# First weight piece in two column halves, a shorter first load of mem^T, and a new order of four evacuations

## Chip, cores and metric

One core of a Trainium2 chip runs the kernel. The metric is the device time of one execution in microseconds (us); lower is better.

## What is computed

The reference is one layer of a decoder trunk on 256 tokens of width 1024. Cut to what the change touches:

```
h    = rmsnorm(x, g_pre_mix)
proj = h @ w_in                      # columns: conv B|C|V, q, k, v, memory q, three gates
o    = moba_attention(q, k, v)       # 8 heads x 64, causal, with a position bias
kv   = rmsnorm(mem, g_mem) @ w_mem_kv        # 256 memory tokens: mk | mv, 512 columns each
y_c  = softmax(qm @ mk^T * 128**-0.5) @ mv   # 4 heads x 128
```

After that come gates, an output projection, a second rmsnorm and a gated MLP with a depthwise convolution. They are not touched.

## The kernel before, in words

**Arithmetic.** Every float32 operand of a matrix product is split into two float32r parts: `hi` is a copy made by ScalarE (ACT), `lo` is the difference made by VectorE (DVE). A product is hi·hi + hi·lo + lo·hi, three matmuls on TensorE (PE). Weights are split as they are used: `split_until` (L202) makes `wh` (L211, ACT) and `wl` (L212, DVE) of one piece; there are five buffers of each, and a piece is split three pieces ahead of the block that uses it (`weights`, L215; two ahead in v's loop).

**Pieces.** All weights lie in one DRAM tensor in the order of use (`weight_pieces`, L56). Pieces 0 to 7 are the eight k-tiles of mem's value weights (128 x 512 each), 8 to 11 mem's key weights, 12 to 15 v's weights, 16 to 19 q's, 20 to 23 k's (128 x 1024 each).

**Start.** SyncE's queue issues w0, w1, ... (one DMA a piece, L410 to L420), ScalarE's queue issues two loads of `gmT` (L132): the gain of mem and k-tiles 0 and 1 of mem^T, then k-tiles 2 and 3; SyncE brings the rest. `keep_warm` (L425) runs nine matmuls on a constant while the data comes. For k-tile 0 of mem^T the DVE makes both parts (L434, L435), for the others ACT and DVE (`mem_part`, L430). Inside the block that starts at L421 the order on PE, ACT and DVE is the order in which the code is written: w0's parts, mem^T's k-tile 1, w1's parts, k-tile 2, and so on. The first product of piece 0 is L445, of the pieces after it L251 (`mm_ktile` by way of `values`, L405).

**The stage that is reordered.** After mem's values (accumulated in `pmv`), mem's keys (`mk_raw`) and v (accumulated in `pv`, L464 to L468), the block goes on: the norms of mem's rows (`rm`, L469), the parts of mem's values scaled by `rm` (`mv`, L472), the diagonal matrices of `rm` (`dg`, L296), their spread over all partitions by a matmul with ones (`spread`, L299: PE writes `sp`, L303, DVE copies it, L305), and the scaled keys (`mk`, L476, L477). There the hand-written order ends. Behind it, in the order of the code but placed by the framework's own planner, come v's parts (`vk`, L490), four blocks of q and four of k. A block (`wide_blocks`, L352) takes a PSUM bank, runs 8 matmuls with `wh` (L237) and 8 with `wl` (L239); ACT copies half of the bank (`t`, L244) and DVE adds (`y`, L245). After each second block `q_evac` (L499) makes four instructions (L502 on ACT, L503 on DVE, for two halves of the partitions).

**PSUM.** `bank()` (L112) gives tiles of the tag "mm", four buffers: the banks of `ft` (the blocks), `sp` and, later, `po` (the attention's output, L560) are all of this tag. `pmv`, `pv`, the scores and the transposes of the attention are of the tag "acc", four buffers.

Of the kernel before, what the change touches and what calls it, by code (L numbers as in the profile page):

```python
# [11 lines left out]
F32 = mybir.dt.float32  # L12
F32R = mybir.dt.float32r
BF16 = mybir.dt.bfloat16
AF = mybir.ActivationFunctionType
ALU = mybir.AluOpType
# [3 lines left out]
P = 128  # L20
# [76 lines left out]
def trunk(ctx, tc, x, mem, memT_in, weights_in, par_in, bias_in, g_post_mix, g_post_ffn, out):  # L97
# [8 lines left out]
    def tok(t):  # L106
        return slice(t * P, (t + 1) * P)

    def f32(ap):
        return ap.bitcast(F32)  # L110
# [18 lines left out]
    gp, gf, bg, cw = par[:, 0:8], par[:, 8:16], par[:, 16:40], par[:, 40:52]  # L129
    fw = par[:, 52:].rearrange("p (a b) -> p a b", a=2)  # L130
    with tc.manual_schedule(engines={mybir.EngineType.Activation}):
        for a, b in ((0, KT + 2 * S), (KT + 2 * S, KT + 4 * S)):  # L132
            nc.scalar.dma_start(gmT[:, a:b], memT_in[:, a:b])
    ident = const.tile([P, P], F32, name="ident")
    ones = const.tile([P, P], F32, name="ones")
# [34 lines left out]
    def raw_tile(g):  # L170

        if g not in lent:
            return wp.tile([P, 2048], F32, tag="raw", name="raw", bufs=RAWS)
        tag, j = lent[g]
        if tag not in lent_tiles:
            lent_tiles[tag] = sb.tile([P, 2 if tag == "C" else 1, 2048], F32, tag=tag, name="rawx")
        return lent_tiles[tag][:, j]

    def load(first, last):

        g = load_of[first]
        if len(raws) == g:
            raws.append([raw_tile(g), 0])
        o = offs[loads[g][0]]
        a, b = offs[first], offs[last] + pieces[last][2] * pieces[last][4]
        nc.sync.dma_start(raws[g][0][:, a - o:b - o], weights_in[:, a:b])
        raws[g][1] += last + 1 - first

    def load_until(n):
        for g in range(min(n, len(loads))):  # L190
# [11 lines left out]
    def split_until(n):  # L202
        while len(parts) < min(n, len(pieces)) and (
                len(parts) in extra or sum(i not in extra for i in range(freed, len(parts))) < PARTS):
            i = len(parts)
            g = load_of[i]
            load_until(ahead_of(g))
            _, _, a, _, b = pieces[i]
            o = offs[i] - offs[loads[g][0]]
            v, hi, lo = (w[:, :a * b].rearrange("p (a b) -> p a b", b=b) for w in [raws[g][0][:, o:]] + part_tiles(i))  # L210
            nc.scalar.activation(hi, v, AF.Copy)  # L211
            nc.vector.tensor_tensor(lo, v, f32(hi), ALU.subtract)  # L212
            parts.append((hi, lo))
# [44 lines left out]
    def hilo(hi, lo, src, scale=1.0):  # L258

        nc.scalar.activation(hi, src, AF.Copy, scale=scale)  # L260
        if isinstance(scale, float) and scale == 1.0:
            nc.vector.tensor_tensor(lo, src, f32(hi), ALU.subtract)
        else:
            nc.vector.scalar_tensor_tensor(lo, src, scale, f32(hi), op0=ALU.mult, op1=ALU.subtract)
# [20 lines left out]
    def rstd_row(src, name):  # L285
        ss, se, r = small("ss"), small("se"), small(name)
        junk = wk.tile([P, D], F32, tag="pT", name="junkd", bufs=2)
        nc.scalar.activation(junk, src, AF.Square, scale=D ** -0.5, accum_out=ss)
        nc.gpsimd.tensor_scalar(se, ss, EPS, None, op0=ALU.add)
        nc.gpsimd.tensor_tensor(r, se, mhalf, op=ALU.pow)  # L290
        return r
# [92 lines left out]
    def run(gen):  # L384
        for _ in gen:
            pass
# [20 lines left out]
            mm_ktile([(pv[t], 0)], wh, wl, a[:, 0, k, tok(t)], a[:, 1, k, tok(t)], k == 0, k == KT - 1)  # L407

    with tc.manual_schedule(engines={mybir.EngineType.SP}):
        for what in "w0 w1 w2 w3 m46 w4 w5 m68 w6 w7 w8 x0 x1 w9 p w10 w11 w12 w13 t0 t1".split():  # L410
            if what[0] == "m":
                a, b = (KT + int(c) * S for c in what[1:])
                nc.sync.dma_start(gmT[:, a:b], memT_in[:, a:b])
            elif what == "p":
                nc.sync.dma_start(par, par_in)
            elif what[0] == "w":
                load(int(what[1:]), int(what[1:]))
            else:
                t = int(what[1])
                nc.sync.dma_start((x_sb if what[0] == "x" else m_sb)[:, t], (x if what[0] == "x" else mem)[tok(t)])  # L420
    with tc.manual_schedule(engines={mybir.EngineType.PE, mybir.EngineType.Activation, mybir.EngineType.DVE}):  # L421
        nc.scalar.activation(small("preload"), mhalf, AF.Exp)
        pw = bank("pw")

        def keep_warm(n):  # L425
            one = nc.const_aps.tensor(1.0, (P, 512), BF16)
            for _ in range(n):
                nc.tensor.matmul(pw, one[:, :P], one, start=True, stop=True)

        def mem_part(k):  # L430
            hilo(memT[:, 0, k], memT[:, 1, k], rawT[:, k], gm[:, k:k + 1])

        keep_warm(9)
        nc.vector.tensor_scalar_mul(memT[:, 0, 0], rawT[:, 0], gm[:, 0:1])  # L434
        nc.vector.scalar_tensor_tensor(memT[:, 1, 0], rawT[:, 0], gm[:, 0:1], f32(memT[:, 0, 0]), op0=ALU.mult,  # L435
                                       op1=ALU.subtract)
        split_until(1)
        mem_part(1)
        split_until(2)
        for k in range(KT):  # L440
            wh, wl = weights(ahead=1)
            if k == 0:
                for n, (a, w) in enumerate(((0, wh), (1, wh), (0, wl))):
                    for t in range(NT):
                        nc.tensor.matmul(pmv[t], memT[:, a, 0, tok(t)], w[:, 0], start=(n == 0), stop=False)  # L445
            else:
                values(pmv, memT, k, wh[:, 0], wl[:, 0])
            if k + 2 < KT:
                mem_part(k + 2)
                split_until(k + 3)  # L450
        rx = [rstd_row(x_sb[:, 0], "rx")]
        split_until(9)
        rx.append(rstd_row(x_sb[:, 1], "rx"))
        for t in range(NT):
            nc.vector.tensor_scalar_mul(xn[:, t], x_sb[:, t], rx[t])
            split_until(10 + t)
        gen = blocks(4, memT, mk_evac)
        next(gen)
        next(gen)
        scaled(hT, turned(xn, range(0, 4)), gp)  # L460
        next(gen)
        scaled(hT, turned(xn, range(4, KT)), gp)
        run(gen)
        pv = acc("pv")  # L464
        for k in range(0, KT, 2):
            wh, wl = weights(ahead=2)
            for j in range(2):
                values(pv, hT, k + j, wh[:, j], wl[:, j])  # L468
        rm = [rstd_row(m_sb[:, t], "rm") for t in range(NT)]  # L469
        mv = sb.tile([P, 2, NT, CW], F32R, tag="E", name="mv")  # L470
        for t in range(NT):
            hilo(mv[:, 0, t], mv[:, 1, t], pmv[t], rm[t])  # L472
        rms = spread(diagonals(rm), "rms")
        mk = sb.tile([P, 2, HM, S], F32R, tag="mk", name="mk")
        for b, y in zip(range(0, HM, 2), mk_raw):
            nc.vector.tensor_tensor(y, y, twice(rms), ALU.mult)  # L476
            hilo(mk[:, 0, b:b + 2], mk[:, 1, b:b + 2], y)  # L477
        nc.vector.tensor_scalar_mul(bgh, bg, 0.5)


    vk = sb.tile([P, 4, 1024], F32R, tag="A", name="vk")
    vp = vk[:, :2].rearrange("p a (t c) -> p a t c", c=CW)
    kl = vk[:, 2:].rearrange("p j (n s) -> p j n s", s=S)
    bias = sb.tile([P, H, S], F32, tag="bias", name="bias")
    with tc.manual_schedule(engines={mybir.EngineType.Pool}):
        for j, r in enumerate((slice(0, DH), slice(DH, P))):
            nc.gpsimd.memset(f32(kl[r, 1 - j]), 0.0)
        nc.gpsimd.dma_start(bias, bias_in)
    for t in range(NT):
        hilo(vp[:, 0, t], vp[:, 1, t], pv[t])  # L490

    qk = sb.tile([P, 2, 4, 2, S], F32R, tag="C", name="qk")
    q2, k2 = qk[:, 0], qk[:, 1]
    HEAD = (slice(0, DH), slice(DH, P))

    def q_evac(b, p):  # L499
        for j, r in enumerate(HEAD):  # L500
            hi, src = q2[r, b:b + 2, j], p[r]
            nc.scalar.activation(hi, src, AF.Copy, scale=DH ** -0.5)  # L502
            nc.vector.scalar_tensor_tensor(q2[HEAD[1 - j], b:b + 2, j], src, DH ** -0.5, f32(hi), op0=ALU.mult,  # L503
                                           op1=ALU.subtract)

    def k_evac(b, p):
        for j, r in enumerate(HEAD):
            hi, src = k2[r, b:b + 2, j], p[r]
            nc.scalar.activation(hi, src, AF.Copy)
            nc.vector.tensor_tensor(kl[r, j, b:b + 2], src, f32(hi), ALU.subtract)  # L510
            nc.vector.tensor_copy(k2[HEAD[1 - j], b:b + 2, j], f32(hi))

    run(wide_blocks(4, hT, q_evac))
    run(wide_blocks(4, hT, k_evac))


# [338 lines left out]
```

## Time and profile before

| what | us |
|---|---|
| median of 3 runs | 447.78 (447.72 to 448.78) |
| profiled execution | 447.71 |
| its span, first to last instruction | 445.8 |
| PE busy in the span | 434.2 |
| DVE busy | 358.2 |
| ACT busy | 292.5 |

The difference between the profiled execution and its span, 1.9 us, lies outside of the instructions. In rows of a timeline the columns are: start, duration of the group, engine, line, operation, tiles, shape, count, and in brackets the idle time before and what ended it.

### The profile page before, as it was taken

How to read it: one execution, taken by the hardware profiler on the slowest of the kernel's cores; microseconds unless marked ns; L12 is line 12 of the kernel's file. 1: busy time of each engine (PE TensorE's matmuls, PEld its weight loads, DVE VectorE, ACT ScalarE, POOL GpSimd, SP SyncE). 2: the span in 40 equal slices, each digit the busy share in tenths (PEclk: the TensorE clock that was granted, in tenths of full speed). 3: DMA queues.
4: the chain of work that ended last, by engine and by line, in shares of the span. 5: the costliest groups of instructions: out<-in, count | busy, mean ns of one | idle time of the engine just before them, and what ended most of it. 6: DMA issues, size and time to landing. Idle time of an engine off the chain costs nothing.

```text
span 445.8 us, 6664 instructions
## 1 busy us (share of the span) xinstructions
PE 434.2 (97%) x2423; PEld 375.4 (84%) x2423; DVE 358.2 (80%) x634; ACT 292.5 (66%) x526; POOL 13.2 (3%) x35
## 2 busy tenths in 40 slices
PE   8998999999999999999999899999999999999994
PEld 4997888888888988888888698888888888888883
DVE  5787889869986787798686679997879878878875
ACT  6787676757677766666655568866657657657642
POOL 0121000000000000000000300000000000000001
PEclk9999999999999999999999999999999999999998
DMA  8997454543535453455857046556556546546102
GB/s 273 410 419 295 150 191 161 190 160 128 185 122 196 156 187 109 177 190 190 278 193 285 1 159 224 185 188 201 187 182 200 190 176 202 190 175 206 79 1 94
DMA packets 14288, 83.38 MB, mean 187 GB/s; under 512 B 1584, under 2 KB 2096, under 8 KB 5424
## 3 DMA queue, kind: packets, MB, share of 16 engines
q1 hardware_dynamic: 13536, 80.34, 50.5%
q10 hardware_dynamic: 576, 1.58, 1.1%
q0 software_dynamic: 144, 1.05, 0.6%
q8 instruction: 19, 0.31, 0.3%
q14 instruction: 13, 0.11, 0.1%
HBM read 81.91 MB, written 1.05 MB: 186 GB/s over the span
## 4 chain that ended last, share of the span: by engine, by line
PE 95%; ACT 1%; DVE 1%; DMA 1%; issue 0%; POOL 0%; POOLq 0%; DVEq 0%; ACTq 0%
PE ft L237 42%; PE ft L239 21%; PE pf L251 13%; PE po L251 5%; PE pmv L251 2%; PE pv L251 2%; PE po L256 1%; DMA raw<-in_weights_dram 1%; PE ft L229 1%; PE ft L228 1%; PE ft L230 1%; PE at L256 1%; ACT wh L211 1%; PE tp L315 1%; PE ft L377 0%
## 5 line engine op out<-in xcount | busy, mean ns | idle before, releaser
L211 ACT ACTIVATE wh<-raw 128x1024 fp32r<-128x1024 f32 (+1 forms) x139 | 143.3, 1034 | 103.7 <-PE ft L237 71.5
L212 DVE TENSOR_TENSOR wl<-raw,wh 128x1024 fp32r<-128x1024 f32 (+1 forms) x139 | 165.4, 1192 | 53.5 <-ACT wh L211 51.7
L237 PE MATMUL ft<-hT,wh 128*128 128x512 f32 x384 | 97.3, 393 | 0.0
L237 PE MATMUL ft<-h2T,wh 128*128 128x512 f32 x328 | 82.2, 392 | 0.0
L237 PEld LDWEIGHTS ft<-hT,wh 128*128 128x128 f32 x384 | 68.9, 189 | 12.2
L237 PEld LDWEIGHTS ft<-h2T,wh 128*128 128x128 f32 x328 | 59.5, 189 | 11.0
L239 PEld LDWEIGHTS ft<-hT,wl 128*128 128x128 f32 x384 | 52.2, 190 | 3.7
L239 PE MATMUL ft<-hT,wl 128*128 128x256 f32 x384 | 53.6, 282 | 0.0
L244 ACT ACTIVATE t<-ft 128x256 f32<-128x256 f32 x116 | 42.9, 372 | 10.4 <-PE ft L239 10.3
L251 PE MATMUL pf<-wh,f 128*128 128x512 f32 x176 | 49.2, 390 | 0.0
L239 PEld LDWEIGHTS ft<-h2T,wl 128*128 128x128 f32 x328 | 44.9, 190 | 3.3
L239 PE MATMUL ft<-h2T,wl 128*128 128x256 f32 x328 | 45.9, 282 | 0.0
L251 PEld LDWEIGHTS pf<-wh,f 128*128 128x128 f32 x176 | 32.4, 188 | 6.2
L245 DVE TENSOR_TENSOR y<-ft,t 128x256 f32<-128x256 f32 x68 | 28.2, 419 | 2.9 <-ACT t L244 2.6
L251 PE MATMUL pf<-wl,f 128*128 128x512 f32 x88 | 27.5, 390 | 0.0
L748 ACT ACTIVATE u<-v,par 128x256 f32<-128x256 f32 x44 | 24.0, 589 | 3.8 <-DVE v L742 3.8
L597 DVE SCALAR_TENSOR_TENSOR u<-v,par,u 128x255 f32<-128x255 f32 x44 | 19.7, 479 | 0.7 <-ACT u L748 0.7
L598 DVE SCALAR_TENSOR_TENSOR u<-v,par,u 128x254 f32<-128x254 f32 x44 | 19.7, 478 | 0.1
L251 PEld LDWEIGHTS pf<-wl,f 128*128 128x128 f32 x88 | 16.5, 188 | 3.5
L245 DVE TENSOR_TENSOR v<-ft,t 128x256 f32<-128x256 f32 x44 | 18.0, 418 | 0.5 <-ACT t L244 0.5
L251 PE MATMUL po<-wh,mg 128*128 128x512 f32 x64 | 17.9, 389 | 0.0
L251 PEld LDWEIGHTS po<-wh,mg 128*128 128x128 f32 x64 | 11.9, 188 | 2.4
(175 smaller groups left out, 534.8 us busy)
## 6 DMA issues: line engine op xcount, KB each, us to landing
raw<-in_weights_dram SPq DMA_DIRECT2D x66, 1024.0 KB, 4.8
raw<-in_weights_dram SPq DMA_DIRECT2D x8, 256.0 KB, 5.4
rawx<-in_weights_dram SPq DMA_DIRECT2D x4, 512.0 KB, 9.0
rawx<-in_weights_dram SPq DMA_DIRECT2D x2, 1024.0 KB, 12.5
raw<-in_weights_dram SPq DMA_DIRECT2D x2, 512.0 KB, 7.3
x_sb<-in_x_dram SPq DMA_DIRECT2D x2, 512.0 KB, 7.4
m_sb<-in_mem_dram SPq DMA_DIRECT2D x2, 512.0 KB, 9.8
bias<-in_bias_dram POOLq DMA_DIRECT2D x1, 1024.0 KB, 8.9
```

The costliest lines, as they stand in the source:

```text
L211: nc.scalar.activation(hi, v, AF.Copy)
L212: nc.vector.tensor_tensor(lo, v, f32(hi), ALU.subtract)
L228: nc.tensor.matmul(dst, wh[:, k], ah[:, k], start=(k == 0), stop=False)
L237: nc.tensor.matmul(p, wh[:, k], a[:, :, k], start=(k == 0), stop=False)
L239: nc.tensor.matmul(p[:, :S], wl[:, k], a[:, 0, k], start=False, stop=(k == kt - 1))
L244: nc.scalar.activation(t, p[:, S:], AF.Copy)
L245: nc.vector.tensor_tensor(dst, p[:, :S], t, ALU.add)
L251: nc.tensor.matmul(d, a, w[:, c:c + 512], start=(first and w is wh and a is ah), stop=(last and a is al))
L256: nc.tensor.matmul(dst, a[i], b[j], start=(first and n == 0), stop=(last and n == 2))
L597: nc.vector.scalar_tensor_tensor(t[:, 1:], src[:, :S - 1], w1, t[:, 1:], op0=ALU.mult, op1=ALU.add)
L598: nc.vector.scalar_tensor_tensor(t[:, 2:], src[:, :S - 2], w0, t[:, 2:], op0=ALU.mult, op1=ALU.add)
L748: nc.scalar.activation(d, v[:, i], AF.Identity, bias=bb, scale=w2)
```

## The change

Three parts. Piece 0 is loaded by two DMAs of 256 columns each (`load_half`), split in halves (`split_halves`), and its six matmuls of 512 columns become twelve of 256. The first load on ScalarE's queue brings the gain and k-tile 0 of mem^T alone, the second k-tiles 1 to 3. And inside the block of hand-written order, v's parts and the first two blocks of q (with their evacuations and the weight splits that they ask for) now stand ahead of mem's values (`mv`), the diagonals, the spread and mem's keys (`mk`).

```
-        for a, b in ((0, KT + 2 * S), (KT + 2 * S, KT + 4 * S)):
+        for a, b in ((0, KT + S), (KT + S, KT + 4 * S)):
             nc.scalar.dma_start(gmT[:, a:b], memT_in[:, a:b])
...
+    def load_half(i):
+        if not raws:
+            raws.append([raw_tile(0), 1])
+        c = slice(i * 256, i * 256 + 256)
+        nc.sync.dma_start(raws[0][0][:, c], weights_in[:, c])
+
+    def split_halves():
+        hi, lo = (w[:, :512].rearrange("p (a b) -> p a b", b=512) for w in part_tiles(0))
+        for c in (slice(0, 256), slice(256, 512)):
+            nc.scalar.activation(hi[:, 0, c], raws[0][0][:, c], AF.Copy)
+            nc.vector.tensor_tensor(lo[:, 0, c], raws[0][0][:, c], f32(hi[:, 0, c]), ALU.subtract)
+        parts.append((hi, lo))
...
-        for what in "w0 w1 w2 w3 m46 w4 w5 m68 w6 w7 w8 x0 x1 w9 p w10 w11 w12 w13 t0 t1".split():
+        for what in "h0 h1 w1 w2 w3 m46 w4 w5 m68 w6 w7 w8 x0 x1 w9 p w10 w11 w12 w13 t0 t1".split():
...
-        split_until(1)
+        split_halves()
         mem_part(1)
         split_until(2)
...
             if k == 0:
-                for n, (a, w) in enumerate(((0, wh), (1, wh), (0, wl))):
-                    for t in range(NT):
-                        nc.tensor.matmul(pmv[t], memT[:, a, 0, tok(t)], w[:, 0], start=(n == 0), stop=False)
+                for c in (slice(0, 256), slice(256, 512)):
+                    for n, (a, w) in enumerate(((0, wh), (1, wh), (0, wl))):
+                        for t in range(NT):
+                            nc.tensor.matmul(pmv[t][:, c], memT[:, a, 0, tok(t)], w[:, 0, c],
+                                             start=(n == 0 and c.start == 0), stop=False)
...
         rm = [rstd_row(m_sb[:, t], "rm") for t in range(NT)]
+        vk = sb.tile([P, 4, 1024], F32R, tag="A", name="vk")
...
+        for t in range(NT):
+            hilo(vp[:, 0, t], vp[:, 1, t], pv[t])
+        gen = wide_blocks(4, hT, q_evac)
+        next(gen)
+        next(gen)
         mv = sb.tile([P, 2, NT, CW], F32R, tag="E", name="mv")
         for t in range(NT):
             hilo(mv[:, 0, t], mv[:, 1, t], pmv[t], rm[t])
...
         nc.vector.tensor_scalar_mul(bgh, bg, 0.5)
...
-    for t in range(NT):
-        hilo(vp[:, 0, t], vp[:, 1, t], pv[t])
...
-    run(wide_blocks(4, hT, q_evac))
+    run(gen)
     run(wide_blocks(4, hT, k_evac))
```

## Rows read from the trace of the kernel before

**Rows 1.** The page, part 1: busy us, share of the span, instructions.
```profile
PE 434.2 (97%) x2423; PEld 375.4 (84%) x2423; DVE 358.2 (80%) x634; ACT 292.5 (66%) x526; POOL 13.2 (3%) x35
```
**Rows 2.** Waits of PE: who for whom, us in total, times, longest.
```profile
PE sp L303 <- DVE dg L296: 1.3, 1, 1.3
PE pmv L445 <- ACT wh L211: 1.2, 1, 1.2
```
**Rows 3.** Timeline of PE around the end of v's products.
```profile
41.37 0.39 PE L251 MATMUL pv<-wh,hT 128*128 128x512 f32 x1
43.06 0.46 PE L303 MATMUL sp<-dg,ones 128*128 128x128 f32 x2 [1.30 <-DVE dg L296]
43.27 2.09 PE L237 MATMUL ft<-hT,wh 128*128 128x512 f32 x8
...
46.15 0.39 PE L237 MATMUL ft<-hT,wh 128*128 128x512 f32 x1
```
**Rows 4.** Timeline of ACT and DVE in the same stretch.
```profile
37.50 1.22 DVE L212 TENSOR_TENSOR wl<-raw,wh 128x1024 fp32r<-128x1024 f32 x1 [1.48 <-ACT wh L211]
...
40.17 1.23 DVE L212 TENSOR_TENSOR wl<-raw,wh 128x1024 fp32r<-128x1024 f32 x1 [1.45 <-ACT wh L211]
...
41.18 1.21 ACT L260 ACTIVATE vk<-pv 128x512 fp32r<-128x512 f32 x2
41.31 1.40 DVE L264 SCALAR_TENSOR_TENSOR mv<-pmv,rm,mv 128x512 fp32r<-128x512 f32 x2
...
42.63 0.47 DVE L296 TENSOR_SCALAR dg<-ident,rm 128x128 f32<-128x128 f32 x2
43.02 1.28 DVE L262 TENSOR_TENSOR vk<-pv,vk 128x512 fp32r<-128x512 f32 x2
```
**Rows 5.** Groups by form, 36 to 60 us: busy us, mean ns; idle before, releaser.
```profile
L211 ACT ACTIVATE wh<-raw 128x1024 fp32r<-128x1024 f32 x9 | 9.5, 1060 | 7.3 <-PE ft L237 6.1 <-ACT junkd L288 0.6 <-PE pv L251 0.6
...
L502 ACT ACTIVATE qk<-y 64x512 fp32r<-64x512 f32 x4 | 2.5, 624 | 0.0
L245 DVE TENSOR_TENSOR y<-ft,t 128x256 f32<-128x256 f32 x5 | 2.1, 418 | 0.0
L503 DVE SCALAR_TENSOR_TENSOR qk<-y,qk 64x512 fp32r<-64x512 f32 x3 | 2.1, 686 | 0.1
```
**Rows 6.** Timeline of PE in the attention of the first head pair.
```profile
85.86 0.50 PE L256 MATMUL po<-pT,vk 128*128 128x512 f32 x1
86.20 2.02 PE L237 MATMUL ft<-hT,wh 128*128 128x512 f32 x8
...
90.84 0.97 PE L256 MATMUL po<-pT,vk 128*128 128x512 f32 x5
```
**Rows 7.** Timeline of the start: DMA issue, ACT, DVE, weight load of PE.
```profile
0.72 0.89 ACTq L133 DMA_DIRECT2D gmT<-in_memT_dram  x2
...
5.30 0.63 ACT L211 ACTIVATE wh<-raw 128x512 fp32r<-128x512 f32 x1 [2.16 <-DMA raw<-in_weights_dram]
5.51 0.35 DVE L434 TENSOR_SCALAR memT<-gmT 128x256 fp32r<-128x256 f32 x1 [4.49 <-DMA gmT<-in_memT_dram]
...
6.52 0.64 ACT L211 ACTIVATE wh<-raw 128x512 fp32r<-128x512 f32 x1 [0.19 <-DMA raw<-in_weights_dram]
...
7.29 0.68 DVE L212 TENSOR_TENSOR wl<-raw,wh 128x512 fp32r<-128x512 f32 x1
...
8.03 0.19 PEld L251 LDWEIGHTS pmv<-wl,memT 128*128 128x128 f32 x1 [0.47 <-DVE wl L212]
```
**Rows 8.** DMA issues: count, KB each, us from issue to landing.
```profile
gmT<-in_memT_dram ACTq DMA_DIRECT2D x1, 256.0 KB, 5.7
```
**Rows 9.** PE's first and last matmuls; a window with the granted clock (1.00 is full).
```profile
0.76 4.00 PE L428 MATMUL pw<-const-bfloat16-1.0 128*128 128x512 bf16 x9 [0.76 <-PEq L844]
...
438.96 0.39 PE L251 MATMUL pf<-wh,f 128*128 128x512 f32 x1
...
441.00:442.00 1.00, 0.00 (x0) 0.00 (x0) 0.83 (x2) 0.00 (x0) 0.14 (x1) 0.89 0.00 0
```

More of the change, by code (lines that the diff above doesn't have):

```diff
@@ L413, in trunk @@
                 nc.sync.dma_start(gmT[:, a:b], memT_in[:, a:b])
+            elif what[0] == "h":
+                load_half(int(what[1]))
             elif what == "p":
@@ L469, in trunk, with q_evac, k_evac @@
         rm = [rstd_row(m_sb[:, t], "rm") for t in range(NT)]
+        vk = sb.tile([P, 4, 1024], F32R, tag="A", name="vk")
+        vp = vk[:, :2].rearrange("p a (t c) -> p a t c", c=CW)
+        kl = vk[:, 2:].rearrange("p j (n s) -> p j n s", s=S)
+        bias = sb.tile([P, H, S], F32, tag="bias", name="bias")
+        with tc.manual_schedule(engines={mybir.EngineType.Pool}):
+            for j, r in enumerate((slice(0, DH), slice(DH, P))):
+                nc.gpsimd.memset(f32(kl[r, 1 - j]), 0.0)
+            nc.gpsimd.dma_start(bias, bias_in)
+        qk = sb.tile([P, 2, 4, 2, S], F32R, tag="C", name="qk")
+        q2, k2 = qk[:, 0], qk[:, 1]
+        HEAD = (slice(0, DH), slice(DH, P))
+        def q_evac(b, p):
+            for j, r in enumerate(HEAD):
+                hi, src = q2[r, b:b + 2, j], p[r]
+                nc.scalar.activation(hi, src, AF.Copy, scale=DH ** -0.5)
+                nc.vector.scalar_tensor_tensor(q2[HEAD[1 - j], b:b + 2, j], src, DH ** -0.5, f32(hi), op0=ALU.mult,
+                                               op1=ALU.subtract)
+        def k_evac(b, p):
+            for j, r in enumerate(HEAD):
+                hi, src = k2[r, b:b + 2, j], p[r]
+                nc.scalar.activation(hi, src, AF.Copy)
+                nc.vector.tensor_tensor(kl[r, j, b:b + 2], src, f32(hi), ALU.subtract)
+                nc.vector.tensor_copy(k2[HEAD[1 - j], b:b + 2, j], f32(hi))
+        for t in range(NT):
[3 more added lines that the diff above has]
+        next(gen)
         mv = sb.tile([P, 2, NT, CW], F32R, tag="E", name="mv")
@@ L478, in trunk @@
         nc.vector.tensor_scalar_mul(bgh, bg, 0.5)
[L481 to L488, printed above, removed]
-    for t in range(NT):
-        hilo(vp[:, 0, t], vp[:, 1, t], pv[t])
[L495 to L511, printed above, removed]
-    run(wide_blocks(4, hT, q_evac))
+    run(gen)
     run(wide_blocks(4, hT, k_evac))
```

## Prediction

> **What bounds the kernel now.** First the busy shares: PE is busy for 434.2 of 445.8 us [rows 1], so time is won or lost only where PE waits or runs slower. Second PE's waits: the two that the change aims at are 1.3 us before `sp`, for the diagonals `dg` of DVE, and 1.2 us before the first product, for `wh` [rows 2]. Third the timelines around both.
>
> Around `sp` the reader is to see what stands behind it. PE's last product of v starts at 41.37; matmuls of 512 columns follow each other at 0.24 (eight in 2.09, the last of them 0.39 long), so the next slot is 41.61. `sp` starts at 43.06, 1.45 us late, and q's first block starts only after it, at 43.27 [rows 3], though its weights (piece 16) had been split before piece 18's split at 37.50 [rows 4]. Why did q not go first? `sp` and q's banks are of the same tag, "mm". The attention shows the same habit: one matmul of `po`, also "mm", stands exactly at its place in the code, the next block `ft` follows it at once, and the other five of `po` come 5 us later, when their data is there [rows 6]. So I read: banks of one tag are handed out in the order of the code, and a block behind `sp` cannot start before `sp`'s first matmul has been placed. That is the hinge of this forecast.
>
> At the start, PE's steady run begins at 8.03, when `wl` of piece 1 is there [rows 7]. Before that PE waits more than it works; so what counts there is not the first matmul but this `wl`.
>
> **Part 1, the start.** What is late now: w0 and the first mem^T load are there at 5.30 and 5.51, w1 at 6.52 (ACT waits for the DMA), then `wh` 0.64, and `wl` from 7.29 to 7.97 [rows 7]. The second mem^T load, issued near 1.1, lands 5.7 later, at 6.8 [rows 7, 8]: these four loads, 1 MB, have all landed then. After the change the first pair is half as large, so PE's first product comes earlier, perhaps by 0.5 us; but it is followed by the same waits. The second mem^T load now carries k-tile 1 too and has 384 KB; k-tile 1's `hi` stands on ACT ahead of w1's `wh`, so both the second load and w1 must be there, and these are the last of the same 1 MB. From above: w1 is as early as now, and the chain 6.52 + 0.64 + 0.05 + 0.68 gives 7.89 against 7.97, a gain of 0.1. From below: both land at 6.9, then k-tile 1's `hi` takes no more than the 0.64 of a copy twice as wide, and `wh` and `wl` follow: 8.9, a loss of 0.9. I take +0.3: w1 lands last, near 6.85, and k-tile 1 a little before; 6.85 + 0.64 + 0.05 + 0.68 = 8.22, and a DVE that is asked for two halves in place of one adds some. From 8.03 on PE has no wait up to v's end, so the shift is paid in full. The six extra matmuls of piece 0 fall into PE's waits before 8.03 and cost nothing; without that cover they would cost six weight loads of 0.19 [rows 7], 1.1 us at most. The extra DMA on SyncE's queue delays the issue of the later ones by under 0.5 us, while each of them waits longer for its turn; nothing.
>
> The Trainium skill's page "DMA: Bandwidth & Descriptors", section "Issuing engines are not separate DMA queues", says that DMAs of different issuing engines run on the same 16 DMA engines and interleave. By that the larger second load shares the engines with the second half of w0 and with w1, and my +0.3 stands; if instead each queue had its own rate, this part would be nearer to -0.1.
>
> **Part 2, the order behind v.** What goes: the 1.45 us before `sp` [rows 3]. PE now goes from v into q0 (41.6 to 44.4) and q1 (to 47.2), a block being 2.8 us (43.27 to 46.15, some of it the longer first matmul's) [rows 3]. Their weights, pieces 16 and 17, are split inside v's loop as before.
>
> What is late next: `sp` again. It comes behind q1, and `dg` stands on DVE behind all that was moved ahead of it. Today two weight splits that q0 asks for (pieces 18 and 19) run on DVE at 37.50 and 40.17, while v is multiplied [rows 4]; in the new code they stand behind v's parts, which wait for v's end, and in the hand-written order they cannot go ahead. DVE, from v's end, with durations of [rows 4, 5]:
> - v's `lo` twice (1.28): to 43.1. ACT's copies of v end at 42.4 as now.
> - `wl` 18 and 19 (1.22 each, behind two `wh` of 1.06 on ACT): 43.5 to 45.9.
> - the add of q0 (0.42): to 46.3.
> - `wl` 20, which q1 asks for (1.22; its `wh` on ACT until 46.0): to 47.5.
> - the add of q1, whose last matmul ends near 47.3: 0.37 on ACT is no row here, so at least 0.42 on DVE: to 48.1.
> - `q_evac`: ACT 0.62, then two on DVE of 0.69: to 50.2.
> - mem's values (1.40; ACT's half runs beside `q_evac`'s second `lo`): to 51.6.
> - `dg` (0.24 for the first): 51.85; `sp` some 0.15 later: 52.0.
> So PE stands from 47.2 to 52.0, 4.8 us. With neighbours overlapping by 0.08 each, as the pairs in [rows 4] do, it is 4.4. From above: DVE and ACT idle twice in this chain (for q1 and for `q_evac`'s `hi`), and the planner may fill such holes with the splits of pieces 21 and 22, as it put two splits ahead of mem's values today; each costs up to 1.22, less the hole: 6.8. I take 5.4, half of one such filling. Behind the waiting `sp` on PE stand q2, q3 and all of k; ACT and DVE wait for those, so nothing else of use runs. q2's and q3's weights are ready by then. SyncE's next 1 MB load waits for piece 19's buffer, and so goes from 41.4 to 45.9; the first split that reads it (piece 24) is asked for three blocks after q2, near 60, which is cover enough. GpSimd's zeroing and its load of the bias keep their order behind `rm`. mem's keys and values are first used by the attention over mem, far behind.
>
> **The clock.** A PE that stands for 5 us may also come back slow. At the end of the kernel the last matmul ends at 439.35 and the granted clock falls within the window 441 to 442, about 2.4 us later [rows 9]. The first nine matmuls, 512 columns each, took 4.00 us, 0.44 each, against 0.24 for 512 columns in q's block [rows 3, 9]: the lower of the two levels, 1.2 in place of 2.4 GHz, for the first 4 us of work. If the same comes after this wait, the first 4 us of work cost up to 9 x 0.20 = 1.8 us; if the clock holds, nothing. I take 1.6, as the wait is twice the 2.4 us.
>
> The Trainium skill's "TensorE: Matmul & The Clock Gate", section "Why this matters for your kernels", warns of idle gaps between bursts of matmuls, which bring the clock down. It speaks against this change; no row here shows a fall in mid-kernel, and without it the forecast would be 451.9.
>
> **Sum.** +0.3 (start) - 1.45 (wait removed) + 5.4 (wait added) + 1.6 (clock) = +5.8 on the profiled execution's 447.7, which is 0.07 below the median: 453.5. Its ends: -0.1 - 1.45 + 4.4 + 0 = +2.9 (450.6) and +0.9 - 1.45 + 6.8 + 1.8 = +8.1 (455.8).
>
> **Rivals.**
> A, the other side: `sp` lets q2 pass. Then q2 and q3 (5.6 us) cover `dg`, the wait is gone, and the time is 447.78 - 1.45 + 0.3 = 446.6, or 446.2 if the start gains 0.1. For it: the second half of `sp` is passed by q's blocks today, and the planner places by readiness. Against: the first half is not passed though q0 was ready, and `po` repeats that [rows 3, 6]. It decides at one point: whether a block stands between q1 and `sp` on PE. Chance 0.18.
> B, the splits of pieces 18 and 19 do run under v as today [rows 4]: DVE's chain is 2.4 shorter, the wait 3.0, the clock in doubt: 447.7 + 0.3 - 1.45 + 3.0 = 449.5, with the clock up to 451. For it: their buffers are free by then. Against: the strict order of the block, in which they stand behind v's parts. Chance 0.12.
> The forecast: 0.70.
>
> **Numbers.** A difference under 0.3%, 1.3 us, is about what a measurement of this kernel cannot tell from none. Faster by more needs A with a start that does not lose: 0.11; the rest of A is within: 0.07; B and the forecast are slower: 0.82. The range leaves out A and reaches from below B to the forecast's upper end: 448.0 to 455.8.
>
> **What would show it.** PE's waits name `sp` behind `dg` with 4.4 to 6.8 us, at about 47.5 on PE's timeline, with q0 and q1 ahead of it and q2 at once behind; on DVE, `dg` near 52, behind `q_evac` and mem's values; the granted clock below 1.00 in the microseconds after; the first product near 5.4 and piece 1's `wl` near 8.2. I am wrong if a block of q stands on PE between q1 and `sp`, or if `dg` is there before 48.

## Result, and the profile after

The changed kernel takes 455.68 us (median of 4 executions, 455.22 to 456.18), the kernel before in the same comparison 448.28 (447.72 to 449.02): a ratio of 1.0163 [1.0148, 1.0179], slower. The profiled execution took 455.26 with a span of 453.3, against 447.71 and 445.8. The forecast was 453.5 in a range of 448.0 to 455.8: the direction and the mechanism were right, but each of the three losses was larger than its term, and the range held by 0.1 us.

The busy shares of the changed kernel, as in [rows 1]:

```profile
PE 435.9 (96%) x2429; PEld 377.6 (83%) x2429; DVE 358.4 (79%) x635; ACT 293.0 (65%) x527; POOL 13.2 (3%) x35
```

PE is busy for 1.7 us longer in a span that is 7.5 longer, so most of the loss is waiting. PE's waits, as in [rows 2] (us in total, times, longest):

```profile
PE sp L318 <- DVE dg L311: 6.3, 1, 6.3
...
PE pmv L463 <- DVE memT L451: 0.9, 1, 0.9
PE pmv L266 <- ACT wh L226: 0.8, 1, 0.8
```

The wait for `dg` is still there, 6.3 in place of 1.3. At the start, the one wait of 1.2 has become two of 0.9 and 0.8, and a small one of 0.2 for `wl`. PE's timeline, against [rows 3]:

```profile
41.91 0.39 PE L266 MATMUL pv<-wh,hT 128*128 128x512 f32 x1
42.14 1.98 PE L252 MATMUL ft<-hT,wh 128*128 128x512 f32 x8
...
44.91 2.00 PE L252 MATMUL ft<-hT,wh 128*128 128x512 f32 x8
46.75 1.11 PE L254 MATMUL ft<-hT,wl 128*128 128x256 f32 x8
54.20 0.76 PE L318 MATMUL sp<-dg,ones 128*128 128x128 f32 x2 [6.34 <-DVE dg L311]
54.62 3.71 PE L252 MATMUL ft<-hT,wh 128*128 128x512 f32 x8
```

The reader is to see three things. v's last product starts 0.54 later than before (41.37). q0 and q1 follow v without a gap, then PE stands, and q2 comes only behind `sp`. And q2's eight matmuls with `wh` take 3.71, where those of q1 took 2.00. The granted clock shows why. These are windows of the same kernel; the columns are start and end, length, busy us (and instructions) of PE, PEld, DVE, ACT and POOL, granted clock, DMA share, GB/s:

```profile
51.00:52.00 1.00, 0.00 (x0) 0.00 (x0) 0.94 (x2) 0.95 (x3) 0.00 (x0) 0.66 0.96 401
52.00:54.20 2.20, 0.00 (x0) 0.03 (x1) 2.19 (x5) 0.96 (x2) 0.00 (x0) 0.50 0.40 168
54.20:58.20 4.00, 4.00 (x11) 3.23 (x12) 0.05 (x1) 0.00 (x0) 0.00 (x0) 0.51 0.00 0
58.20:59.00 0.80, 0.80 (x9) 0.80 (x7) 0.00 (x0) 0.57 (x1) 0.00 (x0) 1.00 0.00 0
```

With PE standing since 47.86 the clock falls between 51 and 52 from 1.00 to 0.50 (from 2.4 to 1.2 GHz; the mean of 0.66 puts the fall near 51.3), and it is back only after 4 us of work.

**Where the 7.4 us are.** The last matmul of the kernel starts at 446.33, before at 438.96: +7.37. The start gives 0.54. The slot behind q1 is free at 47.71 (46.75 and eight times 0.12) and `sp` comes at 54.20, 6.49 late in place of 1.45: 5.04. What is left, 1.79, agrees with the clock: from `sp` to the end of q2's `wh` part (54.20 to 58.17) it is 3.97, where 0.21 [rows 3] and q1's 1.84 would have been 2.05, so 1.92. The 0.1 between 1.79 and 1.92 was not traced further.

DVE in the same stretch shows what `dg` stood behind; against [rows 4]:

```profile
42.29 1.38 DVE L277 TENSOR_TENSOR vk<-pv,vk 128x512 fp32r<-128x512 f32 x2 [5.73 <-ACT vk L275]
43.92 2.36 DVE L227 TENSOR_TENSOR wl<-raw,wh 128x1024 fp32r<-128x1024 f32 x2 [0.25 <-ACT wh L226]
46.20 0.42 DVE L260 TENSOR_TENSOR y<-ft,t 128x256 f32<-128x256 f32 x1
46.53 3.49 DVE L227 TENSOR_TENSOR wl<-raw,wh 128x1024 fp32r<-128x1024 f32 x3
49.93 0.42 DVE L260 TENSOR_TENSOR y<-ft,t 128x256 f32<-128x256 f32 x1
51.05 1.39 DVE L508 SCALAR_TENSOR_TENSOR qk<-y,qk 64x512 fp32r<-64x512 f32 x2 [0.70 <-ACT qk L507]
52.45 1.41 DVE L279 SCALAR_TENSOR_TENSOR mv<-pmv,rm,mv 128x512 fp32r<-128x512 f32 x2
53.78 0.47 DVE L311 TENSOR_SCALAR dg<-ident,rm 128x128 f32<-128x128 f32 x2
```

It is the chain of the prediction with one row changed: between the adds of q0 and q1 stand three splits (pieces 20, 21, 22), not one. The start, against [rows 7]:

```profile
5.09 0.93 PE L463 MATMUL pmv<-wh,memT 128*128 128x256 f32 x4 [0.87 <-DVE memT L451]
...
6.26 0.51 ACT L275 ACTIVATE memT<-gmT 128x256 fp32r<-128x256 f32 x1 [0.67 <-DMA gmT<-in_memT_dram]
...
7.18 0.63 ACT L226 ACTIVATE wh<-raw 128x512 fp32r<-128x512 f32 x1 [0.41 <-DMA raw<-in_weights_dram]
...
7.84 0.69 DVE L227 TENSOR_TENSOR wl<-raw,wh 128x512 fp32r<-128x512 f32 x1 [0.56 <-ACT wh L226]
...
8.59 0.19 PEld L266 LDWEIGHTS pmv<-wl,memT 128*128 128x128 f32 x1 [0.54 <-DVE wl L227]
```

The first product comes 0.9 earlier (5.09 against 6.01), yet piece 1's `wh` 0.66 later (7.18 against 6.52), and its `wl` is loaded into PE at 8.59 against 8.03.

### The profile page after: what moved, and what is told of

It reads as the page before. It is cut to its first block, busy times and chain, and to the rows that moved or that the text cites. A ratio compares the mean times of both kernels' runs of the same rounds, so it can differ in the third digit from the quotient of the medians.

```text
span 453.3 us, 6681 instructions
## 1 busy us (share of the span) xinstructions
PE 435.9 (96%) x2429; PEld 377.6 (83%) x2429; DVE 358.4 (79%) x635; ACT 293.0 (65%) x527; POOL 13.2 (3%) x35
## 4 chain that ended last, share of the span: by engine, by line
PE 94%; DVE 2%; DMA 1%; ACT 1%; issue 0%; POOL 0%; SPq 0%; POOLq 0%; DVEq 0%; ACTq 0%
PE ft L252 42%; PE ft L254 21%; PE pf L266 13%; PE po L266 5%; PE pv L266 2%; PE pmv L266 2%; PE po L271 1%; DMA raw<-in_weights_dram 1%; DVE wl L227 1%; PE ft L244 1%; PE ft L243 1%; PE ft L245 1%; PE at L271 1%; ACT wh L226 1%; PE tp L330 1%; PE ft L396 0%
## 5 line engine op out<-in xcount | busy, mean ns | idle before, releaser
L252 PE MATMUL ft<-hT,wh 128*128 128x512 f32 x384 | 98.9, 398 | 0.0
L252 PEld LDWEIGHTS ft<-hT,wh 128*128 128x128 f32 x384 | 70.1, 192 | 12.6
```

Of the source, the lines that this page charges most:

```text
L252: nc.tensor.matmul(p, wh[:, k], a[:, :, k], start=(k == 0), stop=False)
```

## The experiments

Every run is compared with executions of the kernel before on the same chip; those spread from 447.6 to 449.3, which the last section comes back to, so differences below 1 us are read from the traces.

**The two parts, each alone.** One kernel has the new order with the old start:

```
-        for what in "h0 h1 w1 w2 w3 m46 ...
+        for what in "w0 w1 w2 w3 m46 ...
-        split_halves()
+        split_until(1)
...
```

> The new order behind v alone; the start is that of the kernel before. Theory (the wait before sp grows to 6.3 us and the clock falls to 1.2 GHz in it): 448.3 + 6.5 - 1.45 + 1.8 = 455.1, the wait of sp for dg 6.2 to 6.5 us, the granted clock at 0.50 for some us after it, v's last product at 41.4 as before. Rival (the start's shift lengthens the wait, since weight splits and loads are later too): below 454.5, the wait under 6 us.

Measured: 455.41, ratio 1.0169 [1.0149, 1.0190]. v's last product starts at 41.36 as before, and this line of its waits is, but for the line numbers, the same as in the changed kernel:

```profile
PE sp L303 <- DVE dg L296: 6.3, 1, 6.3
```

So the order alone makes the wait, and the later start does not lengthen it. The other kernel has the new start with the old order (the third part of the change undone):

> The two changes of the start alone (halves of piece 0, first mem^T load of one k-tile); the order behind v is that of the kernel before. Theory (wl of piece 1 waits for the whole first megabyte, 0.55 us later, and all of PE is shifted): 448.8, ratio 1.0012, v's last product at 41.9, the wait before sp 1.3 us. Rival (the wait before sp takes up the shift, as dg does not hang on PE): 448.3, ratio 1.000, the wait before sp 0.8 us. Rival 2 (the earlier first product is worth something): 447.8 or less.

Measured: 448.48 (448.30 to 448.71, 11 executions), ratio 1.0001 [0.9992, 1.0010]. In the trace v's last product starts at 41.97, 0.60 later than before, and `sp` waits 1.3 as before. The shift is paid as expected; against the median of before, though, it makes no difference, because executions of before are often 1 us longer than its profiled one and this kernel's are not.

**Is the wait the bank's order?** The spread takes its bank from the other tag, so that a block no longer comes after it in the same ring:

```
 def spread(...)
-        p = bank("sp")
+        p = ps.tile([P, 512], F32, tag="acc", name="sp", bufs=4)
```

> The changed kernel with one edit: spread's bank is of the tag acc in place of mm. Theory (q2 is held back because banks of one tag are given in the order of the code): q2 and q3 go ahead of sp, the wait of 6.3 us is gone, the clock stays at 1.00 after the start, 448.3 + 0.55 - 1.45 = 447.4. Rival (the hand-written order of PE holds q2 back): sp stays right behind q1, 455.7.

Measured: 447.49, ratio 0.9982 [0.9970, 0.9993]. Timeline of PE:

```profile
47.89 2.00 PE L252 MATMUL ft<-hT,wh 128*128 128x512 f32 x8
...
58.11 0.88 PE L254 MATMUL ft<-hT,wl 128*128 128x256 f32 x6
58.82 0.61 PE L318 MATMUL sp<-dg,ones 128*128 128x128 f32 x4
```

With nothing else altered, q2, q3, a block of k and most of a second go first, `sp` comes at 58.82 without a wait, and 8 us are back. The order of the code on PE did not hold q2; the shared tag did. The same edit on the kernel before:

> The kernel before with one edit: spread's bank is of the tag acc in place of mm. Theory (the tag holds q0 back): q0 starts at 41.6, sp comes after at least one block of q, the 1.3 us of wait are gone, 447.1, ratio 0.997. Rival (the hand-written order holds q0 back): sp right behind v with its wait, ratio 1.000.

Measured: 447.11, ratio 0.9973 [0.9963, 0.9984]. Timeline of PE:

```profile
41.59 0.39 PE L251 MATMUL pv<-wh,hT 128*128 128x512 f32 x1
41.81 1.98 PE L237 MATMUL ft<-hT,wh 128*128 128x512 f32 x8
...
46.54 0.60 PE L303 MATMUL sp<-dg,ones 128*128 128x128 f32 x4
```

q0 follows v at once, as the hinge of the prediction says it must where the banks allow it, and the 1.45 us of [rows 3] are gone (the profiled execution takes 446.29, that of before 447.71).

**The clock.** 28 matmuls on a constant fill the gap; they compute nothing that is used:

```
-        def keep_warm(n):
+        def keep_warm(n, pw=pw):
...
         next(gen)
         next(gen)
+        pw = bank("pw")
+        keep_warm(28, pw)
```

> The changed kernel with 28 matmuls on a constant between q1 and the spread (about 6 us of PE; they compute nothing that is used). Theory (the fall of the clock in the wait costs 1.8 us beside the wait itself): the granted clock stays at 1.00 there, the first block behind sp takes 2.8 us in place of 4.7, 455.7 - 1.8 = 453.9. Rival (the block behind sp is slow for another cause, such as its weights): 455.7 or more.

Measured: 453.59, ratio 1.0127 [1.0107, 1.0147], 2.1 below the changed kernel's 455.68. Timeline of PE (the trace holds 27 of the 28), and the window behind the gap, with columns as above:

```profile
47.86 6.30 PE L445 MATMUL pw<-const-bfloat16-1.0 128*128 128x512 bf16 x27
54.35 0.46 PE L318 MATMUL sp<-dg,ones 128*128 128x128 f32 x2 [0.19 <-DVE dg L311]
54.57 2.09 PE L252 MATMUL ft<-hT,wh 128*128 128x512 f32 x8
```

```profile
54.30:57.50 3.20, 3.15 (x19) 2.83 (x20) 0.10 (x1) 0.74 (x1) 0.00 (x0) 1.00 0.00 0
```

`sp` is not earlier (54.35), but the granted clock is 1.00 and the block behind it takes 2.09 in place of 3.71. The clock's term is shown, at 1.7 us between the two profiled executions (455.26 and 453.58) and 2.1 between the medians.

**What the start costs.** The two halves of piece 0 alone, and the shorter first load of mem^T alone:

> Piece 0 in two halves alone; mem^T is loaded as before, order as before. Theory (SyncE's queue and ScalarE's take turns, so one DMA more ahead of w1 puts w1 behind the second mem^T load): the second half lands after 5.3, w1 near 6.9 in place of 6.5, wl of piece 1 ends at 8.3 to 8.6 in place of 7.98, v's last product at 41.7 to 41.9. Rival (only the larger second mem^T load does harm): wl of piece 1 ends at 8.0, v's last product at 41.4.

Measured: 448.84, ratio 1.0009 [1.0000, 1.0019]. Timeline of ACT:

```profile
7.18 0.63 ACT L226 ACTIVATE wh<-raw 128x512 fp32r<-128x512 f32 x1 [0.69 <-DMA raw<-in_weights_dram]
```

> The shorter first load of mem^T alone; piece 0 in one piece, order as before. Theory (k-tile 1 now comes with the 384 KB of the second load, and its hi stands on ACT ahead of w1's wh): that hi starts at 6.8 in place of 5.8, wl of piece 1 ends at 8.6 to 8.8, v's last product at 42.0. Rival (the loss of the start comes from the halves alone): wl of piece 1 ends at 8.0, v's last product at 41.4.

Measured: 448.23, ratio 0.9997 [0.9988, 1.0006]. Timeline of ACT:

```profile
4.53 0.63 ACT L211 ACTIVATE wh<-raw 128x512 fp32r<-128x512 f32 x1 [1.39 <-DMA raw<-in_weights_dram]
6.69 0.51 ACT L260 ACTIVATE memT<-gmT 128x256 fp32r<-128x256 f32 x1 [1.53 <-DMA gmT<-in_memT_dram]
7.10 0.61 ACT L211 ACTIVATE wh<-raw 128x512 fp32r<-128x512 f32 x1
```

Either edit alone pushes piece 1's `wh` from 6.52 to 7.1 or 7.2, in one case because w1 itself lands later, in the other because mem^T's k-tile 1, which stands ahead of it on ACT, does; v's last product then starts at 41.97 and 41.83. So each has nearly the full price by itself, and together they cost no more. In the changed kernel it is w1 that comes last: its `wh` waits for the DMA, with k-tile 1 done at 6.77. The medians don't separate either from before. The second run shows one thing more: w0's `wh` starts at 4.53, against 5.03 to 5.32 in five traces with the old start, though nothing was changed on SyncE's queue.

**Can the order be mended?** First, the splits of pieces 18 and 19 are put back under v, where they ran before:

```
+        split_until(20)
         vk = sb.tile([P, 4, 1024], F32R, tag="A", name="vk")
```

> The changed kernel with one edit: the weight splits of pieces 18 and 19 are written ahead of v's parts, so that they run while v is multiplied, as before. Theory (DVE's queue ahead of dg sets the wait, but behind q1's end at 47.9 there stay an add, q's parts and mem's values in any case): the wait for dg is 4.4 to 4.8 us in place of 6.3, 453.8 to 454.3 if the clock still falls. Rival (the two splits set no part of it): the wait stays 6.3, 455.7.

Measured: 455.73, ratio 1.0168 [1.0143, 1.0192]; `sp` still waits 6.3. I had expected 4.4 to 4.8, a miss. Timeline of DVE in this kernel:

```profile
38.53 1.23 DVE L227 TENSOR_TENSOR wl<-raw,wh 128x1024 fp32r<-128x1024 f32 x1 [1.81 <-ACT wh L226]
40.88 1.23 DVE L227 TENSOR_TENSOR wl<-raw,wh 128x1024 fp32r<-128x1024 f32 x1 [1.12 <-ACT wh L226]
...
45.69 0.42 DVE L260 TENSOR_TENSOR y<-ft,t 128x256 f32<-128x256 f32 x1 [1.86 <-ACT t L259]
46.64 3.50 DVE L227 TENSOR_TENSOR wl<-raw,wh 128x1024 fp32r<-128x1024 f32 x3 [0.52 <-ACT wh L226]
```

And of ACT:

```profile
45.27 0.38 ACT L259 ACTIVATE t<-ft 128x256 f32<-128x256 f32 x1 [2.17 <-PE ft L254]
45.55 2.94 ACT L226 ACTIVATE wh<-raw 128x1024 fp32r<-128x1024 f32 x3
```

The two splits run at 38.53 and 40.88, and DVE now waits 1.86 for q0's copy instead. ACT makes piece 20's `wh` only behind that copy (`t`, 45.27), which waits for q0 itself. So the splits of 18 and 19 set no part of the wait: the three splits behind q0's add do, and the first of them waits for ACT, not for DVE.

Second, the splits of pieces 21 and 22 are held behind the spread:

```
         rms = spread(diagonals(rm), "rms")
+        split_until(22)
```

> The changed kernel with one edit: the split of piece 21 is written behind the spread, so that the planner cannot put the splits of pieces 21 and 22 ahead of dg. Theory (what made the wait longer than the 4.8 us of the hand-written chain is these two splits, which delay the add of q1 by 1.6 us): add of q1 near 48.3, dg near 52.2, the wait 4.6 to 4.9 us, 455.7 - 1.6 = 454.1. Rival (the chain through q's parts sets it with or without them): the wait stays 6.3, 455.7.

Measured: 456.08, ratio 1.0174 [1.0153, 1.0195]. Timeline of ACT and DVE, then PE's waits:

```profile
48.03 0.38 ACT L259 ACTIVATE t<-ft 128x256 f32<-128x256 f32 x1 [1.46 <-PE ft L254]
48.45 0.42 DVE L260 TENSOR_TENSOR y<-ft,t 128x256 f32<-128x256 f32 x1 [0.56 <-ACT t L259]
...
52.30 0.47 DVE L311 TENSOR_SCALAR dg<-ident,rm 128x128 f32<-128x128 f32 x2
```

```profile
PE sp L318 <- DVE dg L311: 4.7, 1, 4.7
PE po L271 <- ACT pT L275: 1.6, 1, 1.6
```

The wait is as expected, 4.7: without the filling the prediction's chain (4.8) was right within 0.1. ACT's copy of q1 stands for 1.46 us until q1's last matmul is done, so what lies on DVE ahead of q1's add counts for nothing here; the 4.7 us are what stands behind q1 itself (its copy, its add, q's parts, mem's values, `dg`). The time is not: 1.6 us come back as a wait of the attention for ACT (`pT`), at 93.16 on PE, which the changed kernel does not have. That total was a miss. Why `pT` is late is open: DVE, with the two splits put off, is 2.3 us busier between 56 and 93 than in the changed kernel, but right before `pT` ACT stands for 1.2 us at a copy (`t`, 91.37) that waits for a block of PE.

**A version that beats both.** The kernel before with the diagonals and their spread ahead of mem's values, and nothing else:

```
+        rms = spread(diagonals(rm), "rms")
         mv = sb.tile([P, 2, NT, CW], F32R, tag="E", name="mv")
         for t in range(NT):
             hilo(mv[:, 0, t], mv[:, 1, t], pmv[t], rm[t])
-        rms = spread(diagonals(rm), "rms")
```

> The kernel before with one edit: the diagonals and the spread stand ahead of mem's values in the hand-written order (they need the norms alone). Theory (PE waits for dg only because dg stands behind mem's values on DVE): sp follows v's last product without a wait, 448.5 - 1.4 = 447.1, ratio 0.997. Rival (dg is late because of the norms): the wait stays over 1 us, ratio 1.000.

Measured: 446.36, ratio 0.9963 [0.9950, 0.9977]. Timeline of PE:

```profile
42.56 0.39 PE L251 MATMUL pv<-wh,hT 128*128 128x512 f32 x1
42.79 0.38 PE L303 MATMUL sp<-dg,ones 128*128 128x128 f32 x2
```

`sp` follows v's last product by 0.23, the plain step of a matmul; the wait is gone and no other takes its place. With the changed start added:

> The diagonals and the spread ahead of mem's values, together with the changed start (piece 0 in halves, the shorter first mem^T load). Theory (the two parts add up; the changed start costs 0.6 us against an execution of before whose clock rises early, but its clock always rises early): 447.0 with little spread, ratio 0.997. Rival (the changed start is free once sp has no wait): 446.3.

Measured: 447.01, ratio 0.9971 [0.9961, 0.9981]. It keeps most of the gain and gives about 0.7 back, near the price of the start. With the old start and `keep_warm(12)` in place of `keep_warm(9)`:

> The kernel before with the diagonals and the spread ahead of mem's values, and twelve matmuls on the constant in place of nine at the start. Theory (the executions of the kernel before and of before_dg_first that are 1 us longer are those in which the clock rises only at 9.4, since PE stands from 4.8 to 6.0): the clock rises before 6.5 in all, every run near 446.3, ratio 0.995 to 0.996. Rival (the 1 us has another cause): runs stay spread over 446.2 to 447.6, as with nine.

Measured: 446.25 (446.15 to 446.53, six executions), ratio 0.9952 [0.9938, 0.9965], the lowest median of all. Against the 446.36 with nine, the gain is in the spread: none of the six is a long one.

## Why the prediction was right, and where its sizes were off

**The hinge held.** Banks of one tag go out in the order of the code, so no block stood between q1 and `sp`. Rival A, `sp` letting q2 pass, did not happen; where the tag was changed so that it could, the time was 447.49, 0.9 above A's 446.6. In that run's profiled execution (447.54) v's last product is 0.73 later than before, where A had 0.3 for the start, and `po` waits 0.7 for `pT`, which A had at nothing.

**Start, +0.3: it was +0.54.** The first product came even earlier than the 5.4 of the prediction, and that it would not count was right. Piece 1's `wl` was done at 8.53 (7.84 and 0.69) where the sum had 8.22, since w1's `wh` started at 7.18, not 6.85. What was undersized is the extra DMA's place ahead of w1, which I costed at nothing for the loads behind it: the halves alone move w1's `wh` to 7.18. Why one DMA more for the same bytes does that, no run here shows. A load on ScalarE's queue does delay one on SyncE's: with the first mem^T load made shorter and SyncE's queue as before, w0's `wh` starts at 4.53, in five traces with the old start at 5.03 to 5.32. The Trainium skill's "DMA: Bandwidth & Descriptors", section "Issuing engines are not separate DMA queues", says that such DMAs run on the same 16 engines and interleave. This trace agrees, by 0.5 to 0.8 us, so the other value of -0.1, which hung on queues with rates of their own, falls.

**Wait, 5.4 in place of 1.45: it was 6.5.** The step that failed is half a filling by the splits of pieces 21 and 22. The planner put both ahead of q1's add, which starts at 49.93 in place of 48.45 without them, so the filling cost 1.6 us (6.3 against 4.7), not 0.6. A second step was wrong without harm: the splits of 18 and 19 stood on DVE where the chain had them, 0.4 later, but moving them away changed nothing. The chain ought to have started from ACT: q0's end, its copy, `wh` of piece 20; and without the filling from q1's end. So rival B was also mispriced: it took 2.4 us off the chain, though the prediction's own row lets q1's add wait for q1's last matmul. Had B come true, the time would not have been 449.5 but near the 455.73 of the run that forces it.

**Clock, 1.6: it was 1.8**, the upper end of its bound. The prediction's +1.6 was right in kind: a granted clock of 0.50 from near 51.3 through the first 4 us of work behind the gap. Its condition, a wait of twice the 2.4 us read at the end of the kernel, rested on one reading: in the four traces with this gap PE had stood for 2.6 to 4.8 us when the clock fell, so at the 4.8 us of the bare chain the term would have been partly luck. The warning in the Trainium skill's "TensorE: Matmul & The Clock Gate", section "Why this matters for your kernels", against idle gaps between bursts of matmuls held here, in a gap of 6.3 us.

The three, 0.24, 1.1 and 0.2, add up to the 1.5 by which the last matmul's delay of 7.37 exceeds the forecast's sum of 5.85. All three errors lie on the same side; the range held because its upper end has each of them at its worst.

## What to carry to other kernels

Before work is moved ahead of a small matmul that others must pass, look whether its result tile shares a ring of buffers with the work behind it: a late tile holds every later tile of its tag, and another tag was worth 8 us in the changed kernel (455.68 to 447.49) and 1.4 in the kernel before (447.71 to 446.29, profiled executions). Of two chains that wait for the same engine, put the short one that releases PE first (two 0.24 us diagonals ahead of 1.4 us of values), not more PE work ahead of both. And an earlier first matmul is worth nothing where the steady run starts at a later piece: ask what the extra transfer delays.

## What the hardware showed that was not expected

At the start the clock does not rise at the same moment in every execution. The profiled execution of the kernel with the diagonals first (447.33, of executions from 446.22 to 447.56) began so:

```profile
0.77 4.00 PE L428 MATMUL pw<-const-bfloat16-1.0 128*128 128x512 bf16 x9 [0.77 <-PEq L844]
6.06 2.04 PE L445 MATMUL pmv<-wh,memT 128*128 128x512 f32 x4 [1.30 <-ACT memT L260]
```

Its first four products take 2.04, where the profiled execution of before, with the same code there, had 1.17:

```profile
6.01 1.17 PE L445 MATMUL pmv<-wh,memT 128*128 128x512 f32 x4 [1.25 <-ACT wh L211]
```

The clock's record in the trace, which begins with the rise (the windows print 1.00 ahead of it), has it at 9.41 in place of 4.87, and v's last product is 1.19 later. With twelve constant matmuls:

```profile
0.76 4.76 PE L428 MATMUL pw<-const-bfloat16-1.0 128*128 128x512 bf16 x12 [0.76 <-PEq L844]
6.06 1.16 PE L445 MATMUL pmv<-wh,memT 128*128 128x512 f32 x4 [0.54 <-DVE memT L434]
```

Here the rise is at 4.85, while PE still works, and six executions lie within 0.4 us. PE stands between the constant matmuls and the first product in the kernel before too, and that is the likely source of its spread of 447.6 to 449.3; a longer execution of before itself was not traced, so this is argued, not shown. It would also explain how the changed start can cost 0.6 us in the trace and nothing in the median: alone, its first product follows the constant matmuls sooner (at 4.76, without a gap, in the profiled execution), and its executions lie within 0.4 us. But the clock is not the only source of the spread. The changed kernel, with the same start, spreads over 0.96 us, and with the diagonals first this start spreads over 0.8: there the longest execution is the profiled one (447.69), its clock has risen at 3.80, and PE loses time in a wait of 0.45 for a weight split at 21.86.
